# Pinning ScalarE's operand splits behind earlier work in layer 0's attention

## The chip, the cores and the metric

The kernel runs on one core of a Trainium2 chip. The metric is the device time of one execution in microseconds. A core has five engines that run at the same time, each through a stream of instructions of its own, in order: TensorE (PE: matmuls, with its weight loads shown as PEld), VectorE (DVE), ScalarE (ACT), GpSimd (POOL) and SyncE (SP), which here issues nearly all DMA transfers. They wait for one another through semaphores. Matmul results land in PSUM, in banks of 512 float32 values per partition; everything else lives in SBUF.

## The reference

Two post-norm decoder layers on a sequence of 1024 positions and a width of 1024. Layer 0 mixes tokens by differential attention, layer 1 by forgetting attention; a gated MLP with a short convolution follows each. The change touches layer 0's attention alone:

```python
q, k, v = jnp.split(x @ w_qkv, 3, axis=-1)
q = apply_rotary(q.reshape(B, S, H, 2, d), cos, sin, PARTIAL_ROT).transpose(0, 2, 3, 1, 4)
k = apply_rotary(k.reshape(B, S, H, 2, d), cos, sin, PARTIAL_ROT).transpose(0, 2, 3, 1, 4)
v = v.reshape(B, S, H, 2 * d).transpose(0, 2, 1, 3)
...
s = jnp.einsum('bhcqd,bhckd->bhcqk', qb, k) * scale
p = masked_softmax(s, causal_mask(start, Q_BLOCK, S))
a = (p[:, :, 0] - lam * p[:, :, 1]).astype(v.dtype)
o = jnp.einsum('bhqk,bhkd->bqhd', a, v)
o = rms_norm(o, subln_g) * (1.0 - lambda_init)
```

There are 8 heads of two score maps each (`d` = 64).

## The kernel before

**Split operands.** Each product runs as three matmuls in a rounded 32-bit format (`mm3`, L99 to L101). For it every operand is split into a high and a low part: ScalarE copies the source into the rounded type (L88), VectorE subtracts that copy from the source (L90). So each split is one ScalarE and one VectorE instruction, and in the profile all splits share these two lines: `wh` and `wl` are the halves of a weight slab, `q` and `t` those of queries and keys, `pt` those of transposed probabilities, `xh` and `xl` those of activations.

**Slabs.** Layer 0's projection weights come as 24 slabs of 128x1024 (three per head: q, k, v), then 8 slabs of the output weight. `ahead(i)` has SyncE fetch slab i into a staging tile `wst` (L108); `ready(i)` splits it (`cut`). There are two `wst` buffers. The second score map's probabilities of each query tile use the same two.

**The attention loop.** `attention` goes over 8 heads (called pairs, since each has two score maps). While a pair's attention runs, the next pair's projection (`project`) is threaded through it as a generator of 48 steps, each one k tile of a matmul group. It takes q, k and v for the two sequence halves in the order (q,0), (k,0), (q,1), (k,1), (v,0), (v,1). `after(n, fn)` puts a piece of work n steps ahead. The steps that matter here, by the order number n and with i = 3p: fetch slab i+2 at n = 1 and i+3 at n = 4; split i+1 three steps after n = 0 begins, i+2 three steps after n = 2, i+3 three steps after n = 5; fetch i+4 at n = 5.

**Rotary.** Projected q and k are evicted to SBUF by ScalarE (L430). SyncE gathers the rotated rows into a small tile (`gather`, L455 and L457), VectorE turns them (`turn`, L464 to L466), SyncE writes them back (L470). Then `halves` splits q (`split_q`) and k (`split_k`), each half-sequence at a time, and SyncE copies parts of the result to where the score matmuls want them (`move`, L265).

**Attention proper.** For each query tile and map: score matmuls (L507, L508), a masked minimum on VectorE (L510), the exponential on ScalarE (L532), and scaling or combination on VectorE (L537, L542). PE transposes the combined probabilities (L1347) into a PSUM bank (`m`, four buffers), the transposed tile is split (`pt`), and `products` multiplies it with V. `diff_values` normalizes (ScalarE L554 to L559 and L577 to L579, VectorE L560 and L581 to L583, PE L567 and L568). `turn_v` transposes the projected V on PE (L476) into another `m` bank.

**What sets the order.** The source is traced in one order. A scheduler then lays each engine's stream out by a model of when operands will be ready, and may put an instruction ahead of others of the same engine that were traced before it. It also hands out the buffers. On the chip each engine follows the stream it was given.

Of the kernel before, what the change touches and what calls it, by code (L numbers as in the profile page):

```python
# [10 lines left out]
F32R = mybir.dt.float32r  # L11
BF16 = mybir.dt.bfloat16
I32 = mybir.dt.int32
AF = mybir.ActivationFunctionType
# [9 lines left out]
NP = 8  # L24
# [14 lines left out]
W_CUT = 3  # L39
# [16 lines left out]
class Trunk:  # L56
# [25 lines left out]
    def tmp(self, dt=F32, pool=None, tag="t", **k):  # L82
        return (pool or self.tp).tile([P, 1024], dt, tag=tag, name=self.nm(tag), **k)

    def split(self, hi, lo, src, scale=None):

        nc = self.nc
        nc.scalar.activation(hi, src, AF.Copy, scale=1.0 if scale is None else scale)  # L88
        if scale is None:
            nc.vector.tensor_tensor(lo, src, hi.bitcast(F32), op=ALU.subtract)  # L90
        else:
            nc.vector.scalar_tensor_tensor(
                lo, src, scale, hi.bitcast(F32), op0=ALU.mult, op1=ALU.subtract)
# [14 lines left out]
        self.nc.sync.dma_start(st, src)  # L108
        return st

    def cut(self, st, alt=None):
        if alt:
            wh, wl = alt
        else:
            wh = self.wp.tile([P, 1024], F32R, tag="wh", name=self.nm("wh"))
            wl = self.wp.tile([P, 1024], F32R, tag="wl", name=self.nm("wl"))
        self.split(wh, wl, st)
        return wh, wl


# [143 lines left out]
        for dst, src in pairs:  # L264
            self.nc.sync.dma_start(dst.bitcast(F32), src.bitcast(F32))  # L265

    def split_q(self, l, par, src, scale, sl, lo):


        a, b = par[0][:, sl], par[1][:, sl]  # L270
        self.split(a, lo, src, scale)
        hi = slice(0, 64) if l else slice(64, P)
        lo_ = slice(64, P) if l else slice(0, 64)
        self.move((b[hi], a[64:]), (b[lo_], lo[64:]), (a[64:], lo[:64]))

    def split_k(self, l, p, t, src, sl):


        a, b, lo = t[2][:, sl], t[3][:, sl], t[4][:, sl]
        self.split(a, lo, src)  # L280
        self.move((b[64:], a[64:]), (b[:64], a[64:]), (a[64:], a[:64]))
        if l:
            self.move((t[7][:64, sl], lo[64:]))
            if p:
                self.sum_rows(p, t, sl)
# [25 lines left out]
        if i < len(self.slabs):  # L311
            self.stage[i] = self.fetch(self.slabs[i])

    def ready(self, i):
        if i < len(self.slabs):
            self.w[i] = self.cut(self.stage.pop(i))

    def first_loads(self):

# [73 lines left out]
    def project(self, l, p, t):  # L393


        dst, r, i = [None] * 3, {}, 3 * p
        order = ((0, 0), (1, 0), (0, 1), (1, 1), (2, 0), (2, 1)) if l == 0 else \
            [(s, c) for s in range(3) for c in range(2)]
        for n, (s, c) in enumerate(order):
            if l == 0:  # L400
                if n in (1, 4):
                    self.ahead(i + 2 + n // 4)
                elif n in (0, 2, 5):
                    self.after(W_CUT, self.ready, i + (1, 0, 2, 0, 0, 3)[n])
                if n == 5 and p < NP - 1:
                    self.ahead(i + 4)
            else:
                (self.ready if c else self.ahead)(i + s + 1)
            if s == 2 and p == NP - 1:
                self.out_ahead(l, c)  # L410
            ps = self.mbank()
            yield from self.dense_steps(ps, *self.w[i + s], c)
            if c == 0 and (l == 0 or s == 2):
                dst[s] = self.tmp()
            self.after(D_EV, self.result, l, p, s, c, ps, dst[s], t)
            if l == 0 and s == 1:
                self.after(D_EV + 1, self.gather, dst, r, c)
                self.after(D_ROT[c], self.turn, dst, r, c)
                for j in range(2):
                    self.after(D_CUT[c][j], self.halves, dst, t, c, j)  # L420
            if s == 2:
                self.after(D_V[c], self.turn_v, l, c, dst[2], *t[5:7], True)
            if c:
                del self.w[i + s]
# [13 lines left out]
    def halves(self, dst, t, c, j):  # L438

        sl = slice(c * 512, c * 512 + 512)  # L440
        if j == 0:
            self.split_q(0, t[:2], dst[0][:, sl], None, sl, dst[0][:, sl].bitcast(F32R))
        else:
            self.split_k(0, 0, t, dst[1][:, sl], sl)

    def gather(self, dst, r, c):

# [1112 lines left out]
```

## Time and profile before

| what | value |
|---|---|
| median of 3 runs | 2461.72 us (2459.13 to 2468.21) |
| profiled execution, its own time | 2468.86 us |
| its span, first to last instruction | 2467.1 us |
| mean granted TensorE clock | 0.994 |
| layer 0's attention with projections | about the first 500 us |
| ScalarE, VectorE busy over the span | 51%, 78% |

A row of the timeline gives start and duration in us, engine, source line, operation, tiles written and read, shapes and the count of merged instructions. In brackets stands how long the engine was idle before it and what ended that idle time. A row of waits gives the waiter, what it waited for, the total in us, how often, and the longest. A row of windows gives the stretch, its length, the busy time of each engine, the granted clock, the share of the DMA engines and GB/s. Matmuls are pipelined, so that their durations overlap: their rate is read from start to start.

### The profile page before, as it was taken

The numbers are of one execution on the slowest core, as the hardware profiler recorded it, in microseconds if no ns is written. First come the engines' busy times: TensorE is split into PE (matmuls) and PEld (weight loads), VectorE is DVE, ScalarE is ACT, GpSimd is POOL, SyncE is SP. The second block draws the span as 40 slices with busy tenths as digits, with TensorE's granted clock in tenths as the row PEclk, the third lists the DMA queues.
The fourth block names the chain that finished last, engine by engine and source line by source line (L and its number), as shares of the span: only waits on it lengthen the run. The fifth ranks groups of instructions, "written<-read, shape, count | busy, mean of one in ns | idle before, by whom it ended". The sixth has DMA issues, their size and how long they took to land.

```text
span 2467.1 us, 33672 instructions
## 1 busy us (share of the span) xinstructions
PE 2415.5 (98%) x11803; PEld 2016.3 (82%) x11803; DVE 1919.3 (78%) x3763; ACT 1263.7 (51%) x2420; POOL 140.4 (6%) x321
## 2 busy tenths in 40 slices
PE   8999999999999999999999999999999999999998
PEld 6888887788888888888778888888888888888886
DVE  5887777899867667887858777778898667678877
ACT  4565565656544444544535555555465444445444
POOL 2111111001000000000101000000010000000000
PEclk9999999999999999999999999999999999999999
DMA  5232222622322323975232222225223222328751
GB/s 174 72 84 81 73 74 74 196 94 95 103 77 79 99 80 98 341 249 171 88 98 65 65 65 65 65 74 171 78 86 111 77 77 79 101 97 325 257 171 69
DMA packets 116035, 283.41 MB, mean 115 GB/s; under 512 B 18108, under 2 KB 25276, under 8 KB 115864
## 3 DMA queue, kind: packets, MB, share of 16 engines
q1 hardware_dynamic: 115064, 279.34, 35.3%
q8 instruction: 93, 1.52, 0.3%
q0 software_dynamic: 800, 1.90, 0.2%
q14 instruction: 78, 0.64, 0.1%
HBM read 188.44 MB, written 59.18 MB: 100 GB/s over the span
## 4 chain that ended last, share of the span: by engine, by line
PE 75%; DVE 10%; DMA 6%; ACT 4%; SPq 2%; issue 2%; DVEq 0%; POOL 0%; ACTq 0%
PE m L99 18%; PE m L101 18%; PE m L100 18%; PE s L99 3%; PE s L100 3%; PE s L101 3%; PE m L1347 3%; DMA wst<-in_w 3%; PE s L508 2%; PE s L507 2%; DVE s L510 1%; DMA pt<-in_wd 1%; PE m L1373 1%; PE m L1372 1%; ACT wh L88 1%
## 5 line engine op out<-in xcount | busy, mean ns | idle before, releaser
L99 PE MATMUL m<-xh,wh 128*128 128x512 f32 x768 | 320.5, 417 | 10.4 <-ACT xh L88 9.2
L101 PE MATMUL m<-xh,wl 128*128 128x512 f32 x768 | 306.5, 399 | 0.5 <-DVE wl L90 0.5
L100 PE MATMUL m<-xl,wh 128*128 128x512 f32 x768 | 304.0, 396 | 0.0
L99 PE MATMUL m<-xh,wo 128*128 128x512 f32 x656 | 255.6, 390 | 1.1 <-DVE xl L90 0.9
L100 PE MATMUL m<-xl,wo 128*128 128x512 f32 x656 | 255.2, 389 | 0.0
L101 PE MATMUL m<-xh,wo 128*128 128x512 f32 x656 | 255.2, 389 | 0.0
L510 DVE CUSTOM_DVE_ANT_0 s<-s,mask 128x128 f32<-128x128 f32 (+7 forms) x256 | 194.3, 759 | 41.4 <-PE s L508 40.5
L88 ACT ACTIVATE wo<-wg 128x512 fp32r<-128x512 f32 x168 | 106.3, 633 | 223.4 <-PE m L101 215.2
L88 ACT ACTIVATE pt<-m 128x512 fp32r<-128x512 f32 (+1 forms) x240 | 128.7, 554 | 121.7 <-PE m L1347 87.2
L99 PE MATMUL m<-q,wo 128*128 128x512 f32 x472 | 184.0, 390 | 0.0
L100 PE MATMUL m<-q,wo 128*128 128x512 f32 x472 | 183.6, 389 | 0.0
L101 PE MATMUL m<-q,wo 128*128 128x512 f32 x472 | 183.6, 389 | 0.0
L99 PEld LDWEIGHTS m<-xh,wh 128*128 128x128 f32 x768 | 146.5, 191 | 33.8 <-ACT xh L88 9.2
L101 PEld LDWEIGHTS m<-xh,wl 128*128 128x128 f32 x768 | 146.2, 190 | 32.9 <-DVE wl L90 1.6
L90 DVE TENSOR_TENSOR pt<-m,pt 128x512 fp32r<-128x512 f32 (+1 forms) x240 | 148.6, 633 | 21.4 <-ACT pt L88 19.4
L100 PEld LDWEIGHTS m<-xl,wh 128*128 128x128 f32 x768 | 147.1, 192 | 22.2 <-DVE xl L90 0.4
L88 ACT ACTIVATE wo<-t 128x512 fp32r<-128x512 f32 x132 | 82.7, 627 | 140.6 <-PE m L101 133.3
L502 POOL CAST qz<-q 64x128 fp32r<-64x128 f32 x256 | 97.8, 383 | 879.8 <-PE s L508 849.5
L99 PEld LDWEIGHTS m<-xh,wo 128*128 128x128 f32 x656 | 123.1, 188 | 27.6 <-PE m L939 1.4
L90 DVE TENSOR_TENSOR wo<-wg,wo 128x512 fp32r<-128x512 f32 x168 | 115.3, 687 | 38.0 <-ACT wo L88 37.2
L101 PEld LDWEIGHTS m<-xh,wo 128*128 128x128 f32 x656 | 123.1, 188 | 25.8
L100 PEld LDWEIGHTS m<-xl,wo 128*128 128x128 f32 x656 | 123.1, 188 | 25.4
(337 smaller groups left out, 6052.6 us busy)
## 6 DMA issues: line engine op xcount, KB each, us to landing
wst<-in_w SPq DMA_DIRECT2D x46, 512.0 KB
t<-in_wi SPq DMA_DIRECT2D x44, 512.0 KB
ha<-ad SPq DMA_DIRECT2D x88, 256.0 KB
wg<-in_wi SPq DMA_DIRECT2D x42, 512.0 KB
ad<-t SPq DMA_DIRECT2D x42, 512.0 KB
q<-q SPq DMA_DIRECT2D x128, 128.0 KB
pt<-in_wd SPq DMA_DIRECT2D x24, 512.0 KB
hb<-in_wd SPq DMA_DIRECT2D x44, 256.0 KB
```

Of the source, the lines that this page charges most:

```text
L88: nc.scalar.activation(hi, src, AF.Copy, scale=1.0 if scale is None else scale)
L90: nc.vector.tensor_tensor(lo, src, hi.bitcast(F32), op=ALU.subtract)
L99: mm(out, wh, xh, start=start, stop=False)
L100: mm(out, wh, xl, start=False, stop=False)
L101: mm(out, wl, xh, start=False, stop=stop)
L502: nc.gpsimd.tensor_copy(qz[r:r + 64, :], q[r:r + 64, qt * P:qt * P + P])
L507: nc.tensor.matmul(sb[:, ks], q[:, qt * P:qt * P + P], kd[:, ks], start=True, stop=False)
L508: nc.tensor.matmul(sb[:, ks], qz[rows], kl[rows, ks], start=False, stop=True)
L510: nc.vector.tensor_tensor_reduce(sb[:, :ln], sb[:, :ln], self.mask[:, S - ln:], 1.0, BIG, ALU.add, ALU.min, mn)
L1347: nc.tensor.transpose(tb[:, w:w + P], self.pts[q][:, kt * P:kt * P + P], k.ident)
L1372: mm(o, self.v[0][:, vs], h, start=first, stop=False)
L1373: mm(o, self.v[0][:, vs], l, start=False, stop=last)
```

## The change

The helper `split` can now pin its ScalarE instruction: an ordering edge, with no semaphore, to the ScalarE instruction traced just before it. The scheduler can then no longer put it ahead of that one. Pinned are, in layer 0's `project`, the three slab splits of each pair, and the q and k splits of `halves`. The fetch of slab i+4 moves from n = 5 itself to one step after the split of slab i+3 is due. For the last pair, the split of its first output slab (i+3) is traced at n = 5 at once and stays unpinned.

```diff
-    def split(self, hi, lo, src, scale=None):
+    def split(self, hi, lo, src, scale=None, pin=False):
...
-        nc.scalar.activation(hi, src, AF.Copy, scale=1.0 if scale is None else scale)
+        i = nc.scalar.activation(hi, src, AF.Copy, scale=1.0 if scale is None else scale)
+        if pin:
+            self.tc.keep_in_program_order(i)
...
-    def ready(self, i):
+    def ready(self, i, pin=False):
         if i < len(self.slabs):
-            self.w[i] = self.cut(self.stage.pop(i))
+            self.w[i] = self.cut(self.stage.pop(i), pin=pin)
...
             if l == 0:
                 if n in (1, 4):
                     self.ahead(i + 2 + n // 4)
+                elif n == 5 and p == NP - 1:
+                    self.ready(i + 3)
                 elif n in (0, 2, 5):
-                    self.after(W_CUT, self.ready, i + (1, 0, 2, 0, 0, 3)[n])
-                if n == 5 and p < NP - 1:
-                    self.ahead(i + 4)
+                    self.after(W_CUT, self.ready, i + (1, 0, 2, 0, 0, 3)[n], True)
+                    if n == 5:
+                        self.after(W_CUT + 1, self.ahead, i + 4)
...
         if j == 0:
-            self.split_q(0, t[:2], dst[0][:, sl], None, sl, dst[0][:, sl].bitcast(F32R))
+            self.split_q(0, t[:2], dst[0][:, sl], None, sl, dst[0][:, sl].bitcast(F32R), True)
         else:
-            self.split_k(0, 0, t, dst[1][:, sl], sl)
+            self.split_k(0, 0, t, dst[1][:, sl], sl, True)
```

`cut`, `split_q` and `split_k` only pass `pin` on. The edit adds four lines, so that later lines have numbers higher by 2 or 4 (L88 stays, L90 becomes L92, L430 becomes L434, L510 becomes L514).

The scheduler lays the streams out anew. Three places of one pair, the one that starts at about 291 us of the trace before; the others look alike.

First, ScalarE around the normalization and the splits of the first half. `q_623` and `q_625` are the high parts of q and k, `wh_752` (then `wh_751`) is the high part of slab i+3. Before:

```order
L577 ACTIVATE m_690_3397<-m_690_3397,eps_rms_315 128x256
L88 ACTIVATE q_623_3129<-t_676_3337 128x512
L578 ACTIVATE m_690_3397<-m_690_3397 128x256
L579 ACTIVATE sr_719_3530<-m_690_3397 128x256
L88 ACTIVATE q_625_3131<-t_700_3439 128x512
L88 ACTIVATE wh_752_3741<-wst_734_3636 128x1024
L554 COPY of_691_3404<-m_724_3564 128x256
```

Now:

```order
L558 COPY of_691_3404<-m_724_3564 128x256
L536 ACTIVATE p_740_3674,ls_730_3603<-s_728_3596,nm_729_3601 128x896
L562 ACTIVATE m_724_3564<-of_691_3404 128x256
L434 ACTIVATE t_700_3439<-m_720_3540 128x512
L563 CAST sq_733_3616<-m_724_3564 128x256
L88 ACTIVATE q_623_3129<-t_676_3337 128x512
L88 ACTIVATE q_625_3131<-t_700_3439 128x512
L88 ACTIVATE pt_745_3702<-m_741_3676 128x512
L536 ACTIVATE wst_747_3708,ls_738_3669<-s_736_3662,nm_737_3667 128x896
L88 ACTIVATE pt_757_3759<-m_748_3710 128x512
L434 ACTIVATE t_749_3720<-m_735_3638 128x512
L88 ACTIVATE wh_751_3739<-wst_734_3636 128x1024
```

The two splits moved behind the copy, an exponential, an eviction and the cast; the slab's split, which stood just ahead of the copy, now stands eleven rows behind it.

Second, ScalarE around the split of slab i+4 (`wh_785`) and the splits of the second half. Before:

```order
L577 ACTIVATE m_724_3564<-m_724_3564,eps_rms_315 128x256
L88 ACTIVATE wh_785_3871<-wst_750_3721 128x1024
L578 ACTIVATE m_724_3564<-m_724_3564 128x256
L579 ACTIVATE sr_762_3774<-m_724_3564 128x256
L88 ACTIVATE pt_774_3820<-m_761_3770 128x384
L88 ACTIVATE q_623_3129<-t_676_3337 128x512
L532 ACTIVATE wst_776_3826,ls_756_3753<-s_754_3746,nm_755_3751 128x1024
L88 ACTIVATE q_625_3131<-t_700_3439 128x512
```

Now they stand here, eleven rows and more further on, in the start of the next pair:

```order
L88 ACTIVATE pt_790_3882<-m_783_3858 128x512
L563 CAST sq_784_3864<-m_756_3752 128x256
L88 ACTIVATE wh_785_3871<-wst_762_3779 128x1024
L88 ACTIVATE pt_798_3912<-m_793_3890 128x512
L536 ACTIVATE p_800_3919,ls_789_3881<-s_787_3876,nm_788_3879 128x256
L88 ACTIVATE q_623_3129<-t_676_3337 128x512
L536 ACTIVATE wst_807_3958,ls_796_3904<-s_794_3899,nm_795_3902 128x256
```

The slab's split stands between the cast and the next probability split, and q's behind the exponential after that.

Third, VectorE ahead of the low part `pt_774`, whose PSUM bank the V transposes on PE reuse. Before:

```order
L465 TENSOR_TENSOR t_702_3450<-t_702_3450,rope_229 128x256
L464 TENSOR_TENSOR t_702_3450<-t_702_3450,rope_229 128x256
L90 TENSOR_TENSOR pt_758_3761<-m_748_3710,pt_758_3761 128x512
L466 TENSOR_TENSOR t_702_3450<-t_702_3450 128x256
L535 RECIPROCAL rs_775_3823<-ls_744_3701 128x1
L537 TENSOR_SCALAR p_760_3768<-p_760_3768,rs_775_3823 128x1024
L90 TENSOR_TENSOR wl_786_3872<-wst_750_3721,wh_785_3871 128x1024
L510 ISA s_754_3746,nm_755_3751<-s_754_3746,mask_294 128x1024
L510 ISA nm_755_3751 128x1
L90 TENSOR_TENSOR pt_774_3820<-m_761_3770,pt_774_3820 128x384
```

Now:

```order
L92 TENSOR_TENSOR pt_757_3759<-m_748_3710,pt_757_3759 128x512
L469 TENSOR_TENSOR t_702_3450<-t_702_3450,rope_229 128x256
L92 TENSOR_TENSOR wl_752_3740<-wst_734_3636,wh_751_3739 128x1024
L468 TENSOR_TENSOR t_702_3450<-t_702_3450,rope_229 128x256
L539 RECIPROCAL rs_775_3823<-ls_744_3701 128x1
L470 TENSOR_TENSOR t_702_3450<-t_702_3450 128x256
L514 ISA s_753_3744,nm_754_3749<-s_753_3744,mask_294 128x1024
L514 ISA nm_754_3749 128x1
L541 TENSOR_SCALAR p_759_3766<-p_759_3766,rs_775_3823 128x1024
L92 TENSOR_TENSOR pt_774_3820<-m_760_3768,pt_774_3820 128x384
```

The low part of slab i+4 is gone from here, that of slab i+3 has come in, the probability split ahead of the rotary steps has moved up, and the minimum now stands ahead of the scaling.

More of the change, by code (lines that the diff above doesn't have):

```diff
@@ L109, in fetch, with cut @@
         return st
-    def cut(self, st, alt=None):
+    def cut(self, st, alt=None, pin=False):
         if alt:
@@ L116, in cut @@
             wl = self.wp.tile([P, 1024], F32R, tag="wl", name=self.nm("wl"))
-        self.split(wh, wl, st)
+        self.split(wh, wl, st, pin=pin)
         return wh, wl
@@ L265, in move, with split_q @@
             self.nc.sync.dma_start(dst.bitcast(F32), src.bitcast(F32))
-    def split_q(self, l, par, src, scale, sl, lo):
+    def split_q(self, l, par, src, scale, sl, lo, pin=False):
         a, b = par[0][:, sl], par[1][:, sl]
-        self.split(a, lo, src, scale)
+        self.split(a, lo, src, scale, pin)
         hi = slice(0, 64) if l else slice(64, P)
@@ L274, in split_q, with split_k @@
         self.move((b[hi], a[64:]), (b[lo_], lo[64:]), (a[64:], lo[:64]))
-    def split_k(self, l, p, t, src, sl):
+    def split_k(self, l, p, t, src, sl, pin=False):
         a, b, lo = t[2][:, sl], t[3][:, sl], t[4][:, sl]
-        self.split(a, lo, src)
+        self.split(a, lo, src, pin=pin)
         self.move((b[64:], a[64:]), (b[:64], a[64:]), (a[64:], a[:64]))
```

## The prediction

> **What bounds the kernel now.** I read the page's first table first: TensorE (PE) is busy nearly all the time.
>
> ```profile
> PE 2415.5 (98%) x11803; PEld 2016.3 (82%) x11803; DVE 1919.3 (78%) x3763; ACT 1263.7 (51%) x2420; POOL 140.4 (6%) x321
> ```
>
> So a change in ScalarE's order is worth what PE idles or is slowed in layer 0's attention. Next, PE's waits in the first 600 us (total us, times, longest us):
>
> ```profile
> PE m L476 <- DVE pt L90: 15.5, 5, 3.2
> PE m L99 <- ACT xh L88: 9.2, 1, 9.2
> PE m L1347 <- DVE pt L90: 2.3, 4, 0.7
> ```
>
> One wait returns five times: PE is about to transpose the first half of V (L476), and the PSUM bank for it is freed by VectorE's half of a probability split (pt, L90). Then busy time by pair of heads (columns: stretch, length, busy us of PE, PEld, DVE, ACT, POOL, granted clock, DMA):
>
> ```profile
> 113.50:170.10 56.60, 55.60 (x305) 47.22 (x304) 46.16 (x114) 35.77 (x82) 7.99 (x16) 1.00 0.32 89
> 170.10:230.00 59.90, 56.72 (x305) 48.56 (x304) 46.42 (x114) 35.79 (x82) 6.67 (x16) 0.97 0.28 76
> 230.00:291.60 61.60, 57.91 (x306) 49.58 (x305) 46.28 (x115) 35.59 (x82) 7.10 (x16) 0.94 0.26 73
> 291.60:351.10 59.50, 56.32 (x305) 48.35 (x304) 46.30 (x114) 35.81 (x81) 5.99 (x16) 0.97 0.27 76
> 351.10:411.70 60.60, 56.69 (x305) 48.44 (x304) 46.32 (x114) 35.75 (x82) 7.03 (x16) 0.97 0.27 75
> 411.70:474.90 63.20, 58.95 (x306) 50.04 (x305) 50.37 (x122) 39.47 (x90) 5.08 (x16) 0.95 0.52 149
> ```
>
> The first of these pairs runs without the wait and at full clock: 56.60 us. The next four have the same matmuls and take 60.4 on average. After each long wait the clock halves, which two stretches behind the wait of the fourth row, and one around a shorter wait elsewhere, show:
>
> ```profile
> 333.90:337.10 3.20, 3.13 (x10) 2.65 (x11) 3.06 (x9) 1.85 (x4) 0.00 (x0) 0.50 0.36 81
> 88.50:98.50 10.00, 7.63 (x41) 5.95 (x41) 9.48 (x18) 7.17 (x15) 0.74 (x2) 1.00 0.35 97
> ```
>
> At half clock 3.2 us of work cost 1.6 us more. In the second row PE idles 2.4 us, but in pieces, and the clock stays at 1.00.
>
> Now back from the wait, in the pair of 291.6 (timelines of PE, VectorE, ScalarE, SyncE):
>
> ```profile
> 333.97 1.12 PE L476 MATMUL m<-ident,t 128*128 128x128 f32 x4 [3.18 <-DVE pt L90]
> ...
> 328.13 0.49 DVE L466 TENSOR_TENSOR t<-t 128x256 f32<-128x256 f32 x1
> 328.54 0.15 DVE L535 RECIPROCAL rs<-ls 128x1 f32<-128x1 f32 x1
> 328.72 0.75 DVE L537 TENSOR_SCALAR p<-p,rs 128x1024 f32<-128x1024 f32 x1
> 331.08 1.23 DVE L90 TENSOR_TENSOR wl<-wst,wh 128x1024 fp32r<-128x1024 f32 x1 [1.61 <-ACT wh L88]
> 332.22 1.23 DVE L510 CUSTOM_DVE_ANT_0 s<-s,mask 128x1024 f32<-128x1024 f32 x1
> 333.37 0.55 DVE L90 TENSOR_TENSOR pt<-m,pt 128x384 fp32r<-128x384 f32 x1
> ...
> 317.50 1.06 ACT L88 ACTIVATE wh<-wst 128x1024 fp32r<-128x1024 f32 x1 [3.33 <-DMA wst<-in_w]
> ...
> 324.73 0.60 ACT L430 ACTIVATE t<-m 128x512 f32<-128x512 f32 x1
> ...
> 329.99 1.06 ACT L88 ACTIVATE wh<-wst 128x1024 fp32r<-128x1024 f32 x1 [2.03 <-DMA wst<-in_w]
> ...
> 326.11 0.53 SPq L108 DMA_DIRECT2D wst<-in_w  x1
> ```
>
> The slab's DMA is issued at 326.11 and lands at 329.99. Its split stands in ScalarE's stream as if it had landed earlier: ScalarE is blocked 2.03 us, VectorE's half (wl) 1.61 us, and behind wl stand the score minimum (L510) and the pt that PE needs. PE was ready at 333.97 - 3.18 = 330.79. An earlier slab blocks ScalarE 3.33 us in the same pair. Among ScalarE's waits from 113 to 475 us:
>
> ```profile
> ACT wh L88 <- DMA wst<-in_w: 26.5, 10, 4.1
> ```
>
> **The change part by part.** No arithmetic is added or removed; the fetch of slab i+4 is traced four steps later, and its SyncE row still stands directly behind the rotary gathers. What moves is the splits.
>
> *Slabs.* The split that blocked 3.33 us now follows L430 at 324.73, 7 us after its landing at 317.50. The one that blocked 2.03 us moves past the wait, into the next pair, behind the square's cast. That cast, like the next pair's rows here, stands at:
>
> ```profile
> 342.17 0.36 ACT L559 CAST sq<-m 128x256 fp32r<-128x256 f32 x1
> 342.74 0.60 ACT L88 ACTIVATE pt<-m 128x512 fp32r<-128x512 f32 x1 [0.21 <-PE m L1347]
> ...
> 350.33 0.48 PE L99 MATMUL m<-xh,wh 128*128 128x512 f32 x1
> ```
>
> Issued near 326.4 (below) and 3.9 us under way, its slab lands near 330.3, over 8 us ahead of the cast even when the cast comes 3 us earlier. Split by 345, it is first needed by the matmul of 350.33. So both blocks of ScalarE go, at no cost of their own.
>
> *What sets the pt now.* VectorE's row of pt now has this ahead of it: minimum (L510), the pt of the tile before, one rotary multiply, wl, the other multiply, reciprocal, the rotary add, minimum, scaling (L537), pt. The chain starts from
>
> ```profile
> 325.10 1.23 DVE L510 CUSTOM_DVE_ANT_0 s<-s,mask 128x1024 f32<-128x1024 f32 x1
> 326.24 0.14 DVE L510 DVE_READ_ACCUMULATOR2_ANT nm<- 128x1 f32 x1
> 326.24 0.42 DVE L465 TENSOR_TENSOR t<-t,rope 128x256 f32<-128x256 f32 x1
> 327.18 0.42 DVE L464 TENSOR_TENSOR t<-t,rope 128x256 f32<-128x256 f32 x1 [0.52 <-DMA t<-t]
> 327.52 0.68 DVE L90 TENSOR_TENSOR pt<-m,pt 128x512 fp32r<-128x512 f32 x1
> ```
>
> I put its start at 325.3, 0.2 later than before, since the q and k splits of the first half (two on VectorE, 0.68 each) now stand ahead of it, where VectorE waited before. From start to start of the rows above: minimum 1.14, pt 0.61, multiply 0.34, wl 1.14, multiply 0.34, reciprocal 0.18, add 0.41, minimum 1.15, scaling 0.75, pt 0.55: 6.6 us. So pt ends at 331.9, and PE, ready at 330.8, waits **1.1 us instead of 3.18**. The five waits average 15.5 / 5 = 3.1 us, so in four pairs that gains 4 x 2.0 = **8.0 us**. Bounds: no wait at all, 12.4 us; 2.5 us of it left, 2.4 us.
>
> *Clock.* The four pairs' clock shares cost 0.03 x 59.9 + 0.06 x 61.6 + 0.03 x 59.5 + 0.03 x 60.6 = 9.1 us, of which about 1 falls inside the waits. I take **8 us** as gained, since waits of about 1 us left the clock at 1.00 above; the other bound is nothing. [...]
>
> *The last pair* keeps one block, because its first output slab is cut unpinned, as before. Of its long wait and its clock (3.1 us, and 0.05 x 63.2 = 3.2 us) I expect less than half to go, **2.5 us**; bounds 0 and 6.3.
>
> *What the moved work collides with.* In the next pair's start VectorE gets wl (1.23) and later the second half's two splits (0.68 each), ScalarE 1.06 + 2 x 0.63, ahead of two pt splits.
>
> ```profile
> 337.00:350.00 13.00, 13.00 (x86) 11.82 (x85) 10.27 (x33) 8.82 (x23) 1.85 (x6) 1.00 0.30 81
> ```
>
> VectorE is idle 2.7 of these 13 us and takes on 2.6. The pt of 342.74 ends some 1.6 us later, about when PE, whose transposes moved behind six products, wants its bank. I charge 0.3 us for each of five pairs, **1.5 us**; bounds 0 and, if none of the 2.6 is hidden, 13.
>
> *SyncE.* The q and k moves now stand behind ScalarE's later splits and ahead of the last gathers. They issue one after the other, about 0.6 us each:
>
> ```profile
> 318.22 0.39 PE L101 MATMUL m<-xh,wl 128*128 128x512 f32 x1
> ...
> 320.01 0.60 ACT L430 ACTIVATE t<-m 128x512 f32<-128x512 f32 x1
> ...
> 321.51 0.66 SPq L455 DMA_DIRECT2D t<-t  x1
> 322.35 0.50 SPq L265 DMA_DIRECT2D q<-q  x1
> ...
> 324.79 1.22 SPq L457 DMA_DIRECT2D t<-t  x2
> ```
>
> Before, the first gather of the second operand started at 321.51, its data there at 320.6, and ScalarE's block had made that late: PE had it at 318.6. Now this gather starts near 319.4, and twelve issues with their waits end near 326.4, against 326.0. The gather lands near 327.6; the multiply that reads it comes at 328.5. Cost 0; without that cover, one for one.
>
> **Sum.** 8.0 + 8 + 2.5 - 1.5 = 17.0 us. The profiled execution took 2468.86 us (span 2467.1, and 1.8 around it), so its like would take 2451.9. The median of the three runs is 2461.72, 7.1 below it. From there it would be 2444.7. Two of the five half-clock stretches of the profiled run are double ones, by the 0.94 and 0.95 rows; a faster run probably has fewer of them to lose, so I forecast **2446 us**.
>
> **The rivals.**
>
> *The wait survives (30%).* VectorE has 6.6 us of work between a fixed start and PE's need. If the start or a row slips by 1.5 us, the wait is again over 2.5 us and the clock still drops. For it: VectorE is busy 15 of the 20 us ahead of this wait, and the gather's landing has under 1 us of margin. Against: both blocks on ScalarE were the wait's last cause. Gain 5 x 0.7 us: 2458.
>
> ```profile
> 313.90:333.90 20.00, 16.90 (x88) 14.03 (x86) 15.08 (x30) 10.96 (x22) 1.29 (x4) 0.99 0.39 108
> ```
>
> *The clock does not recover (7%).* Waits shorten as forecast, but several short waits for banks still halve the clock: then 8.0 + 1 - 1.5 = 7.5 us is left, 2454. The row 88.50:98.50 speaks against it. [...]
>
> *The wait vanishes (13%).* If VectorE reaches pt by 330.8, the five waits (15.5) and their clock (9.1 + 3.2) go: 27.8 less some 2 of overlap, 2436. For it: the pair at 113.50 already runs so. Against: the 6.6 us have no idle time in them.
>
> *SyncE's queue turns against it (8%).* Place: the last gathers, behind moves that wait for pinned splits and for each other's landings. VectorE is in order, so a gather that is late by x us blocks the minimum and pt behind it. The wait becomes 1.1 - 0.9 + x; from x = 3 us it equals the old one, and at x = 6 (three more waits of a move for another's landing, about 2 us each) it is 6.2 instead of 3.1: 5 x 3.1 = 15 us slower, 2477. Against: the moves before waited only 2.3 us in all here.
>
> ```profile
> SPq L265 <- DMA q<-q: 2.3, 1, 2.3
> ```
>
> That the pins do nothing is excluded by the order.
>
> **How the numbers follow.** Forecast 42%, rivals 30, 7, 13 and 8. The range 2435 to 2461 takes in the vanished wait, the forecast, and the surviving wait; outside lie the slow case and tails. About 0.5% (12.3 us, below 2449.4 or above 2474) is what a measurement here can tell from no change. Faster: the vanished wait (0.13), nine tenths of the forecast (0.38) and a little of the two rivals with a smaller gain (0.05): 0.56. Slower: most of SyncE's rival, 0.07. The rest, 0.37, is the same.
>
> **What will show it.** Right: PE's wait at the V transposes near 1 us, granted clock 1.00 in all these pairs, pairs near 56.6, and no long wait of a slab split for its DMA except in the last pair. Wrong: PE waiting over 2.5 us there, VectorE's rotary multiply waiting for a gather, or a new wait at the probability transposes early in a pair.

## The result and the profile after

The changed kernel takes **2445.47 us** (median of 4 runs, 2442.78 to 2448.64), the kernel before 2462.89 us on the same chip (4 runs, 2459.13 to 2468.21). The ratio is **0.9928, 95% interval 0.9905 to 0.9951**: 17.4 us faster. The forecast was 2446 us. The profiled execution took 2448.64 us, with a span of 2446.8.

TensorE has 9.4 us less to do, by the first table of the page after; it ran the same matmuls in less half-clock time (mean granted clock 0.998, before 0.994):

```profile
PE 2406.1 (98%) x11803; PEld 2007.9 (82%) x11803; DVE 1917.5 (78%) x3763; ACT 1264.2 (52%) x2420; POOL 139.7 (6%) x321
```

Busy time by pair of heads, after, cut at the second V transposes of each pair (columns as in the table of before: stretch, length, busy us of PE, PEld, DVE, ACT, POOL, granted clock, DMA):

```profile
114.18:169.12 54.94, 54.94 (x305) 47.05 (x304) 46.03 (x114) 35.83 (x82) 7.06 (x16) 1.00 0.33 92
169.12:224.08 54.96, 54.96 (x306) 47.04 (x304) 46.13 (x115) 35.86 (x82) 7.05 (x16) 1.00 0.30 82
224.08:279.02 54.94, 54.94 (x305) 47.06 (x304) 46.07 (x114) 35.83 (x82) 7.03 (x16) 1.00 0.30 82
279.02:333.94 54.92, 54.92 (x305) 47.04 (x304) 46.02 (x115) 35.85 (x82) 7.05 (x16) 1.00 0.30 82
333.94:388.91 54.97, 54.97 (x305) 47.06 (x304) 46.06 (x115) 35.84 (x82) 7.06 (x16) 1.00 0.29 82
388.91:449.86 60.95, 58.00 (x307) 49.01 (x306) 51.33 (x120) 38.71 (x86) 6.04 (x17) 0.97 0.45 144
```

In the first five rows length and PE's busy time are equal: PE does not wait at all, and the clock is 1.00. The four pairs that took 59.9, 61.6, 59.5 and 60.6 us take 54.9 to 55.0, and the pair that I had called free of the wait (56.6) also loses 1.7. Of PE's waits between 113 and 475 us only these are left (total us, times, longest us):

```profile
PE m L480 <- DVE pt L92: 2.9, 1, 2.9
PE m L101 <- DVE q L92: 0.6, 1, 0.6
```

The 2.9 us is the last pair's. The blocks of ScalarE on input slabs are gone from its list of waits; for a weight slab it now waits only in the last pair and behind it, for output slabs (6.9 us, against 4.5 before):

```profile
ACT wh L88 <- DMA wst<-in_wo: 6.9, 3, 4.2
```

Where the time went shows best in two stretches: the six pairs, and all behind them. First two rows of before, then two of after, then two of a second profiled execution of the changed kernel (the first experiment of the second group below):

```profile
113.55:474.89 361.34, 342.12 (x1825) 292.17 (x1824) 281.80 (x686) 218.14 (x494) 39.87 (x96) 0.97 0.32 90
474.89:2467.10 1992.21, 1972.35 (x9494) 1641.98 (x9492) 1561.54 (x2887) 984.61 (x1798) 79.39 (x176) 1.00 0.36 118
```

```profile
114.18:449.86 335.68, 332.73 (x1827) 284.26 (x1826) 281.64 (x685) 217.93 (x491) 41.30 (x97) 0.99 0.33 95
449.86:2446.80 1996.94, 1973.27 (x9492) 1641.39 (x9490) 1561.36 (x2889) 985.62 (x1801) 80.08 (x175) 1.00 0.36 119
```

```profile
113.51:447.59 334.08, 331.20 (x1828) 283.04 (x1826) 281.47 (x685) 218.33 (x491) 42.30 (x97) 1.00 0.33 95
447.59:2440.00 1992.41, 1972.84 (x9492) 1641.53 (x9490) 1561.63 (x2889) 985.54 (x1801) 80.09 (x175) 1.00 0.36 119
```

The six pairs go from 361.34 to 335.68 us, **25.7 us**; of that, PE's idle time (length less busy) falls from 19.2 to 2.9 us, 16.3, and the other 9.4 is the clock. The first profile after then lost 4.7 us behind the pairs, which the second did not: that is a difference between executions, not the change. How 25.7 us in two profiles and 17.4 us in the medians go together is taken up below.

The chain that PE used to wait for, in the pair that the prediction followed (timelines of VectorE and PE after):

```profile
311.03 1.23 DVE L514 CUSTOM_DVE_ANT_0 s<-s,mask 128x1024 f32<-128x1024 f32 x1
...
312.18 0.69 DVE L92 TENSOR_TENSOR pt<-m,pt 128x512 fp32r<-128x512 f32 x1
312.78 0.41 DVE L469 TENSOR_TENSOR t<-t,rope 128x256 f32<-128x256 f32 x1
313.75 1.23 DVE L92 TENSOR_TENSOR wl<-wst,wh 128x1024 fp32r<-128x1024 f32 x1 [0.55 <-ACT wh L88]
314.89 0.42 DVE L468 TENSOR_TENSOR t<-t,rope 128x256 f32<-128x256 f32 x1
...
317.49 0.55 DVE L92 TENSOR_TENSOR pt<-m,pt 128x384 fp32r<-128x384 f32 x1
...
318.10 0.66 PE L480 MATMUL m<-ident,t 128*128 128x128 f32 x4
```

pt ends at 318.04 and PE transposes at 318.10 without a wait. The chain takes 7.0 us from the minimum at 311.03, and it starts 7.07 us ahead of PE.

### The profile page after: what moved, and what is told of

The parts are those of the page before. It is cut to its first block, busy times and chain, and to the rows that moved or that the text cites. A ratio compares the mean times of both kernels' runs of the same rounds, so it can differ in the third digit from the quotient of the medians.

```text
span 2446.8 us, 33670 instructions
## 1 busy us (share of the span) xinstructions
PE 2406.1 (98%) x11803; PEld 2007.9 (82%) x11803; DVE 1917.5 (78%) x3763; ACT 1264.2 (52%) x2420; POOL 139.7 (6%) x321
## 4 chain that ended last, share of the span: by engine, by line
PE 81%; DVE 8%; DMA 6%; ACT 3%; issue 1%; SPq 1%; DVEq 0%; POOL 0%; ACTq 0%; POOLq 0%
PE m L101 20%; PE m L103 20%; PE m L102 20%; PE m L1351 3%; PE s L101 3%; PE s L102 3%; PE s L103 3%; PE s L512 3%; PE s L511 2%; PE m L1377 1%; PE m L1376 1%; DMA pt<-in_wd 1%; DVE wo L92 1%; DMA wb<-in_wd 1%; DMA t<-od 1%
## 5 line engine op out<-in xcount | busy, mean ns | idle before, releaser
L514 DVE CUSTOM_DVE_ANT_0 s<-s,mask 128x128 f32<-128x128 f32 (+7 forms) x256 | 194.3, 759 | 39.0 <-PE s L512 37.6
L88 ACT ACTIVATE wo<-wg 128x512 fp32r<-128x512 f32 x168 | 106.4, 633 | 226.2 <-PE m L103 216.4
L88 ACT ACTIVATE pt<-m 128x512 fp32r<-128x512 f32 (+1 forms) x240 | 128.5, 553 | 131.1 <-PE m L1351 96.8
L92 DVE TENSOR_TENSOR pt<-m,pt 128x512 fp32r<-128x512 f32 (+1 forms) x240 | 148.4, 632 | 20.1 <-ACT pt L88 17.6
L88 ACT ACTIVATE wo<-t 128x512 fp32r<-128x512 f32 x132 | 82.8, 627 | 140.6 <-PE m L103 133.2
L92 DVE TENSOR_TENSOR wo<-wg,wo 128x512 fp32r<-128x512 f32 x168 | 115.2, 687 | 39.8 <-ACT wo L88 38.9
```

Of the source, the lines that this page charges most:

```text
L88: i = nc.scalar.activation(hi, src, AF.Copy, scale=1.0 if scale is None else scale)
L514: nc.vector.tensor_tensor_reduce(sb[:, :ln], sb[:, :ln], self.mask[:, S - ln:], 1.0, BIG, ALU.add, ALU.min, mn)
```

## The experiments

For the first four kernels, theory A is that the splits that block ScalarE on a slab that has not landed carry the gain, and theory B that the query and key splits, or what stands in VectorE's chain, carry it. The later kernels have theories of their own, which stand with each. No kernel here leaves out any of the computation; one repeats a subtraction. Each group shares its runs of the kernel before: median 2463.39 us for the first four kernels (14 runs), 2458.99 for the next four (9 runs), 2458.84 for the last four (19 runs). "Faster by" is that median less the kernel's. The ratio is not the quotient of the two medians: by it the first kernel gains 5.9 us instead of 8.0, and the others differ by at most 1.6 us. "Six pairs" is the length of the stretch above in the kernel's own profile, between the same marks.

| kernel | median us | ratio to before (95%) | faster by | six pairs |
|---|---|---|---|---|
| slab pins alone | 2455.35 | 0.9976 (0.9963–0.9989) | 8.0 | 348.6 |
| q and k pins alone | 2454.14 | 0.9960 (0.9945–0.9975) | 9.3 | 345.2 |
| slab i+4's pin alone | 2448.40 | 0.9937 (0.9923–0.9952) | 15.0 | 341.8 |
| slab i+3's pin alone | 2457.41 | 0.9973 (0.9961–0.9985) | 6.0 | 349.3 |
| the change again | 2441.48 | 0.9933 (0.9920–0.9945) | 17.5 | 334.1 |
| the change, last pair pinned too | 2438.43 | 0.9920 (0.9907–0.9932) | 20.6 | 332.6 |
| the change less slab i+3's pin | 2448.66 | 0.9963 (0.9950–0.9976) | 10.3 | 341.6 |
| the change, VectorE's subtraction three times | 2448.03 | 0.9956 (0.9943–0.9970) | 11.0 | 339.8 |
| the fetch moved, no pin | 2462.11 | 1.0015 (1.0004–1.0026) | -3.3 | 354.5 |
| the change, q and k pins in the first half | 2445.95 | 0.9954 (0.9939–0.9968) | 12.9 | 338.1 |
| the change, q and k pins in the second half | 2453.32 | 0.9979 (0.9969–0.9989) | 5.5 | 346.6 |
| the change, slab splits a step earlier | 2444.52 | 0.9948 (0.9933–0.9963) | 14.3 | 338.1 |

**Slab pins alone.** The change without the pins on queries and keys:

```diff
-            self.split_q(0, t[:2], dst[0][:, sl], None, sl, dst[0][:, sl].bitcast(F32R), True)
+            self.split_q(0, t[:2], dst[0][:, sl], None, sl, dst[0][:, sl].bitcast(F32R))
-            self.split_k(0, 0, t, dst[1][:, sl], sl, True)
+            self.split_k(0, 0, t, dst[1][:, sl], sl)
```

> The slab splits of the change stay pinned, the q and k splits are free again and go back ahead of the normalization; the moved fetch and the last pair stay as in the change. Theory A (the two slab splits that block ScalarE carry the gain): 14 to 18 us faster than before, the wait at the V transposes under 1 us in the four middle pairs, granted clock 1.00 there. Theory B (VectorE's load ahead of the wait carries it, so the q and k splits must leave that stretch too): the second half's q and k splits stand right behind the wait and the first half's back in idle time, so the gain is under 8 us and a wait over 1.5 us is left.

8.0 us faster by the medians and 5.9 by the ratio, about half of what A needs and near B. The slab blocks are gone, and yet PE waits 1.8 to 2.1 us in five of the six pairs, 0.6 in the first. PE's waits of this kernel in the first 600 us, then VectorE's and PE's timeline in the pair that was followed:

```profile
PE m L480 <- DVE pt L92: 10.4, 6, 2.1
```

```profile
317.57 1.23 DVE L514 CUSTOM_DVE_ANT_0 s<-s,mask 128x1024 f32<-128x1024 f32 x1 [0.26 <-PE s L512]
...
319.99 0.43 DVE L469 TENSOR_TENSOR t<-t,rope 128x256 f32<-128x256 f32 x1 [1.13 <-issue]
321.12 0.43 DVE L468 TENSOR_TENSOR t<-t,rope 128x256 f32<-128x256 f32 x1 [0.70 <-DMA t<-t]
321.46 0.68 DVE L92 TENSOR_TENSOR pt<-m,pt 128x512 fp32r<-128x512 f32 x1
...
326.25 0.55 PE L480 MATMUL m<-ident,t 128*128 128x128 f32 x3 [1.94 <-DVE pt L92]
```

The two rotary multiplies (L469, L468) stand ahead of the 512-wide pt here, and VectorE idles 1.83 us ahead of them: 0.70 us for a gather's data, 1.13 for nothing that the profile shows. In the change that pt stands first and fills this time. The minimum starts 6.7 us ahead of PE's readiness, about as in the change, but the chain takes 8.6 us instead of 7.0. That is a new wait in place of the old one, and A alone does not explain the gain.

**Query and key pins alone.** The kernel before with the last two lines of the change, and nothing else:

```diff
-            self.split_q(0, t[:2], dst[0][:, sl], None, sl, dst[0][:, sl].bitcast(F32R))
+            self.split_q(0, t[:2], dst[0][:, sl], None, sl, dst[0][:, sl].bitcast(F32R), True)
-            self.split_k(0, 0, t, dst[1][:, sl], sl)
+            self.split_k(0, 0, t, dst[1][:, sl], sl, True)
```

> Only the q and k splits are pinned; slabs, fetch and last pair are as before. Theory A: both blocks of ScalarE stay, so the long wait stays at 3 us or more in each pair with its half clock: within 6 us of before, rather slower, since the first half's q and k splits now fill time in which VectorE waited. Theory B: at least 8 us faster.

9.3 us faster: A as stated falls here, and B's 8 us is met. Nine of the ten blocks are still there (first row: ScalarE's waits from 113 to 475 us; then timelines), but the scheduler, which plans around pins, has put the blocked split of slab i+4 behind sr, and PE's transposes now wait, in the four middle pairs, for a bank that sr frees:

```profile
ACT wh L88 <- DMA wst<-in_w: 23.7, 9, 3.4
```

```profile
323.68 1.06 ACT L88 ACTIVATE wh<-wst 128x1024 fp32r<-128x1024 f32 x1 [1.66 <-DMA wst<-in_w]
...
324.07 0.41 DVE L584 SCALAR_TENSOR_TENSOR sr<-m,sr 128x256 f32<-128x256 f32 x1
324.77 1.23 DVE L92 TENSOR_TENSOR wl<-wst,wh 128x1024 fp32r<-128x1024 f32 x1 [0.29 <-ACT wh L88]
...
324.54 0.55 PE L478 MATMUL m<-ident,t 128*128 128x128 f32 x3 [1.14 <-DVE sr L584]
```

PE's waits at the V transposes fall from 15.5 to 9.3 us in all, 3.6 of it still for pt. So here a block costs less, since what frees PE's bank stands ahead of it.

**One slab split at a time.** No query or key pin, and only the split of slab i+4 (traced at n = 0 of the next pair) or of slab i+3 pinned (the second kernel has `n == 5` in the line below):

```diff
-                    self.after(W_CUT, self.ready, i + (1, 0, 2, 0, 0, 3)[n], True)
+                    self.after(W_CUT, self.ready, i + (1, 0, 2, 0, 0, 3)[n], n == 0)
```

> Of all splits only that of slab i+4 is pinned, so the block of 2.0 us is gone and the block of 3.3 us stays. Theory A with the last cause alone: VectorE's chain loses 1.6 us of waiting and 1.2 us of wl ahead of the pt, 2.8 of the 3.2 us of wait, the clock stays full: 14 to 18 us faster. If the earlier block sets the start of the chain as well, 1 to 2 us of wait remain: 10 to 14 us faster, clock 1.00. Theory B: under 5 us.

> Of all splits only that of slab i+3 is pinned, so the block of 3.3 us is gone and that of 2.0 us, last ahead of the wait, stays. Theory A with the last cause alone: wait near 3 us, half clock as before, within 4 us of before. If the earlier block delays the gathers and through SyncE the fetch of the next slab, that slab lands 1 to 2 us earlier and the wait falls to 1 to 2 us with full clock: 8 to 14 us faster. Theory B: within 4 us.

15.0 and 6.0 us faster. The first meets A's 14 us; the second lies between A (within 4 us of before) and the 8 to 14 us of an earlier landing. PE's waits in the first 600 us, of the first and of the second:

```profile
PE m L480 <- DVE sr L586: 4.0, 5, 1.1
PE m L480 <- DVE pt L92: 2.8, 1, 2.8
```

```profile
PE m L480 <- DVE pt L92: 12.3, 6, 2.8
```

The split of slab i+4 is the one whose block the prediction saw as the last cause of the wait, and its pin alone removes most of it: no middle wait is over 1.13 us, and the granted clock of the whole span is 0.999, against 0.998 in the first profile after, which has one half-clock stretch in the six pairs. With i+3's pin alone the waits stay between 1.4 and 2.8 us. 15.0 + 6.0 is more than the 17.4 of the whole, and slab pins together gave 8.0: the parts do not add. Each kernel's streams differ around the pins, as the scheduler orders the neighbours anew; which of these differences makes up the sum was not taken apart.

**The change again, and the last pair pinned too.** In the second kernel the split of the last pair's first output slab is pinned, and traced three steps later, like the others:

```diff
-                elif n == 5 and p == NP - 1:
-                    self.ready(i + 3)
...
-                    if n == 5:
+                    if n == 5 and p < NP - 1:
```

> The changed kernel once more, as the yardstick of the three variants beside it: 2445.5 measured before, so 2443 to 2448 here, with PE's wait at the first V transposes gone in the four middle pairs and 2.9 us in the last.

> The change, and the first output slab's split in the last pair pinned as well (no unpinned split is left). Theory A (the wait is made by the blocked split, in the last pair as in the others): the last pair's wait of 2.9 us shrinks below 1.5 us and its half-clock stretch of 3.4 us (1.7 us of work lost) goes with it, so 2 to 4 us faster than the change. Theory B (the last pair's wait comes from its additional output slabs, which load ScalarE and VectorE more, 39.5 and 50.4 us against 35.8 and 46.3): the wait stays over 2 us, within 1.5 us of the change.

2441.48 us (2441.05 to 2444.48) and **2438.43 us** (2438.23 to 2439.93), five runs each on one chip: the ranges do not touch, and the second is 3.0 us faster, as A said. It beats both kernels. On this chip the kernel before takes some 4 us less as well, so the miss of the 2443 to 2448 expected for the change is the chip's; the ratio is the old one. In the last pair's trace PE's wait of 2.6 to 2.9 us is gone; its six pairs are

```profile
111.82:444.37 332.55, 331.31 (x1829) 283.40 (x1828) 281.57 (x686) 219.54 (x493) 42.82 (x97) 1.00 0.33 97
```

with 1.2 us of idle PE in all.

**The change without slab i+3's pin.**

```diff
-                    self.after(W_CUT, self.ready, i + (1, 0, 2, 0, 0, 3)[n], True)
+                    self.after(W_CUT, self.ready, i + (1, 0, 2, 0, 0, 3)[n], n != 5)
```

> The change without the pin on the split of slab i+3, which goes back to where VectorE had idle time, so VectorE's subtraction of 1.14 us is no longer in the chain ahead of pt. Theory A (the wait is what VectorE's chain ends later than PE arrives, and never below zero): the chain is already early enough, so shortening it gives nothing in the middle pairs: within 2 us of the change, as long as ScalarE's block on that slab (3 us) does not come back ahead of the q and k splits. Theory B (that split's block costs by itself, as in the kernel before): 4 us or more slower than the change.

7.2 us slower than the change: B of this run. VectorE's subtraction has left the chain, and the chain is late all the same. ScalarE, VectorE and PE in the pair that was followed:

```profile
305.50 1.06 ACT L88 ACTIVATE wh<-wst 128x1024 fp32r<-128x1024 f32 x1 [3.11 <-DMA wst<-in_w]
...
314.52 1.22 DVE L514 CUSTOM_DVE_ANT_0 s<-s,mask 128x1024 f32<-128x1024 f32 x1
...
320.80 0.66 PE L480 MATMUL m<-ident,t 128*128 128x128 f32 x4 [1.27 <-DVE pt L92]
```

PE was ready at 320.80 - 1.27 = 319.53, and the minimum that opens the chain started only 5.0 us ahead of it, against 7.07 in the change. ScalarE's exponential behind the block (306.72) starts 12.8 us ahead of PE's readiness, and the same one in the change (303.21) 14.9. So a block of 3.1 us nine microseconds earlier moves the *start* of the chain by 2 us. The run with slab i+4's pin alone, in which slab i+3's split blocks 2.64 us, lies between: its minimum starts 6.0 us ahead.

**VectorE's subtraction for slab i+3 three times.** The same result, written three times:

```diff
-            nc.vector.tensor_tensor(lo, src, hi.bitcast(F32), op=ALU.subtract)
+            for _ in range(max(1, pin)):
+                nc.vector.tensor_tensor(lo, src, hi.bitcast(F32), op=ALU.subtract)
...
-                    self.after(W_CUT, self.ready, i + (1, 0, 2, 0, 0, 3)[n], True)
+                    self.after(W_CUT, self.ready, i + (1, 0, 2, 0, 0, 3)[n], 3 if n == 5 else True)
```

> The change, with VectorE's subtraction for slab i+3 done three times (same result): two more of 1.14 us stand ahead of pt, and the reciprocal and scaling (0.93 us) go behind it, so pt comes 1.35 us later in the four middle pairs, at an unchanged PE. Theory A (pt ended 0.06 us before PE came, so there is no slack): four waits of about 1.3 us, 5 us slower than the change, clock still 1.00 behind them. Theory B (VectorE has slack that the trace does not show): under 2 us slower, no wait over 0.5 us. Theory C (the wait also halves the clock): 10 us or more slower.

6.5 us slower than the change, near the 5 us of A, with pairs of 55.8 to 56.3 us instead of 54.95. But the time is not lost where A put it. The scheduler moved PE's V transposes seven products later, where they wait for nothing, and the loss appears behind them, at the probability transposes (PE's waits from 113 to 455 us):

```profile
PE m L1352 <- DVE p L547: 2.7, 5, 0.5
PE m L481 <- DVE pt L93: 2.0, 1, 2.0
PE m L1352 <- DVE pt L93: 0.7, 4, 0.2
```

These waits make 3.4 of the 5.5 us by which the first five pairs are longer than those of the change beside it. VectorE is busy about 2.0 us more in a pair (48.1 against 46.05), and the pair is 1.1 us longer: about half of the added work is hidden, so that neither A's "no slack" nor B holds as stated. Some 1.9 us of the loss in the profile lies ahead of the six pairs, at a wait of 2.5 us at 96 us.

**The fetch moved, no pin.**

```diff
-                    self.after(W_CUT, self.ready, i + (1, 0, 2, 0, 0, 3)[n], True)
+                    self.after(W_CUT, self.ready, i + (1, 0, 2, 0, 0, 3)[n])
```

and the query and key pins off as in the first experiment. The last pair's first output slab stays traced early, as in the change.

> The kernel before with the fetch of slab i+4 moved as in the change, and no pin at all. Theory A (the pins carry the gain, the fetch merely goes with them): within 4 us of the kernel before, its blocks of ScalarE and the waits of about 3 us still there. Theory B (the later fetch alone unblocks ScalarE, since the scheduler then puts the split later too): 8 us or more faster than before.

3.3 us slower than before: A. Waits of PE from 100 to 460 us, and blocks of ScalarE from 110 to 460 us, are the old ones:

```profile
PE m L480 <- DVE pt L92: 14.2, 5, 3.1
```

```profile
ACT wh L88 <- DMA wst<-in_w: 24.7, 9, 3.3
```

The later fetch alone gains nothing; the pins are needed. The slab pins without the later fetch were not tried.

**Query and key pins in one half of the rows.** `True` becomes `c == 0` in the first kernel and `c == 1` in the second, here and in the line of split_q:

```diff
-            self.split_k(0, 0, t, dst[1][:, sl], sl, True)
+            self.split_k(0, 0, t, dst[1][:, sl], sl, c == 0)
```

> The change with the query and key splits pinned in the first half of the rows only (the second half's four splits unpinned). Theory A (the first half's pins matter, since they set what stands ahead of pt in VectorE's stream): within 3 us of the change, 14 to 19 us faster than before, and no wait over 1 us at the V transposes. Theory B (the second half's pins matter, since they take the 2.6 us block of ScalarE on a rotary gather out of the way): 6 to 11 us faster than before, like the change without any of these pins (8.0).

> The change with the query and key splits pinned in the second half of the rows only. Theory A (the first half's pins matter): 6 to 11 us faster than before, with a wait of 1 to 2 us at the V transposes in the middle pairs. Theory B (the second half's matter): within 3 us of the change, 14 to 19 us faster than before.

12.9 and 5.5 us faster than before. PE's waits of the first, from 113 to 475 us, and of the second in the first 600 us:

```profile
PE m L480 <- DVE pt L92: 2.3, 1, 2.3
PE m L101 <- DVE acc L824: 2.0, 2, 1.1
```

```profile
PE m L480 <- DVE pt L92: 10.3, 6, 2.9
```

With the first half's pins the middle waits are gone (the 2.3 is the last pair's); with the second half's alone all of them stay (1.3 to 2.0 us in the four middle pairs), and the gain, just under A's 6 us, is no larger than with none of these pins. So it is the first half's pins that matter for the wait. They stand ahead of the chain. The first kernel still misses the 14 us that A wanted, and is 4.5 us slower than the change: the last pair takes 62.1 us instead of 59.4, with time at half clock (a granted clock of 0.97 from 394 to 460 us) and new waits on acc, and the other pairs 0.1 to 0.5 us more each.

**Slab splits a step earlier.**

```diff
-W_CUT = 3
+W_CUT = 2
```

> The change with every pinned slab split (and the fetch) one step earlier, so that the split of slab i+4 stands directly behind the second V eviction, near its landing, and blocks ScalarE there for up to 2 us; the query and key pins stay. Theory A (a block costs only where the pt that PE waits for stands behind it; here it stands behind the V transposes' pt): within 3 us of the change. Theory B (any block of ScalarE of that size costs PE time): 5 us or more slower than the change.

3.0 us slower than the change, at the edge of what A allowed, but this run tells nothing about A or B: the fetch moves with the split, the slab had landed, and no block arose (from 113 to 475 us the only slabs that ScalarE waits for are output slabs, 6.2 us).

## Why the prediction was right, and where it was not

**What bounds the kernel: right.** The long wait at the V transposes for pt, behind a split that waits for its slab, was the loss. With the blocks gone, the wait and the half clock behind it went, and the moved fetch alone does not bring that about.

**"PE waits 1.1 us instead of 3.18", 8.0 us for four pairs: undersized.** The wait is zero in all four, 12.4 us, which was my upper bound. The step that failed is the chain's start, which I held at 325.3, 5.5 us ahead of PE's readiness, "0.2 later than before". It now stands 7.07 us ahead. The block of 3.33 us on slab i+3 had delayed this start too, and the run that puts that block back moves it to 5.0. The length was nearly right (6.6 forecast, 7.0 found): 1.1 - 1.6 + 0.4 is just below zero. The same error stands in the SyncE part, where I let the product at 318.22 end the bank that L430 evicts. By the numbers of the tiles that product writes the next slab's bank, and in the trace it signals nothing; the product at 316.18, which does, had filled the evicted one by 316.6. So ScalarE's block had held up the eviction, and all behind it, by some 2 us more than I allowed.

**"Pairs near 56.6": wrong floor.** The pair that I took as undisturbed had 1.0 us of idle PE in it, most of it in waits of 0.2 to 0.4 us, and the pairs of the change take 54.95. The other 0.65 us is time in which the profile has PE busy (55.60 against 54.95); its cause stays open. The four pairs gained 21.8 us, not the 14.8 that 8.0, 8 and four fifths of the collisions' 1.5 make.

**The clock, 8 us: right.** In the four pairs the half-clock stretches of before are

```profile
214.20:217.61 3.41, 3.41 (x13) 3.02 (x12) 3.33 (x9) 1.42 (x4) 0.29 (x1) 0.50 0.63 143
272.23:279.05 6.82, 5.88 (x20) 5.20 (x21) 5.41 (x15) 3.27 (x7) 0.29 (x1) 0.50 0.42 96
333.67:337.08 3.41, 3.11 (x10) 2.63 (x11) 3.27 (x9) 2.08 (x4) 0.00 (x0) 0.50 0.36 81
395.11:398.52 3.41, 3.41 (x12) 2.75 (x11) 2.53 (x8) 1.59 (x5) 0.09 (x1) 0.50 0.42 96
```

and the change has none there: its four rows have 1.00. PE is busy in 15.8 of these 17.1 us, and half of that, 7.9 us, is my estimate of what they cost at 0.50. Over the six pairs the clock gave 9.4 us by the rows above, against the 8 forecast for the four pairs and a part of the last pair's 2.5. The other bound that I gave, nothing, no run shows: in each of the four pairs of before the long wait is followed by a row at 0.50.

**The last pair, 2.5 us: right** (63.15 to 60.95, 2.2 us; 59.39 in the second profile, 3.8), and its reason is borne out: pinning the one split that was left, and tracing it later, is worth 3.0 us more.

**Collisions, 1.5 us: not there.** PE has no wait early in a pair. PE's transposes and VectorE's pt both moved, and the pairs run without any idle time.

**SyncE, cost 0: right for the change.** The multiply at 314.89 follows its predecessor without a wait. The mechanism of that rival shows in part all the same: without the query and key pins VectorE waits 0.70 us for a gather in the same place, of 1.83 us idle, and half the gain is lost.

**The rivals.** In mechanism it was the third, the wait vanishes, which I gave 13%; its price of 25.8 us meets the 25.7 of the six pairs. Its time of 2436 did not come, because I took those 25.8 us off the median, and the profiled execution of before had more to lose than the median run: it lies 6 to 7 us above the medians. The kernel with only the fetch moved, whose waits are those of before, spent 354.5 us in the six pairs of its profile, not 361.3, with three half-clock stretches of 3.41 us there instead of three single and two double ones. The runs fit this: of the 28 runs of the kernel before that stand beside the last eight kernels, the six with a mean granted clock of 0.995 average 2460.6 us and the five with 0.998 2455.3, and the profiled execution of before had 0.994. From 354.5 to the 334.1 and 335.7 of the change is 19 to 20 us, near the measured 17.4; the last 2 us are not settled. So 2446 against 2445.5 is in part two errors that cancel: a wait term too small by 4.4 us, with nothing for the small waits and 1.5 for collisions that did not come, and a base from which I took the profile's clock losses nearly whole. That the two numbers agree to half a microsecond is luck.

## What to carry to other kernels

When a block of an in-order engine is removed, move the whole chain with it, its start too: here a wait of 3.1 us for a transfer, nine microseconds ahead of the start of the chain, had set when the chain began (5.0 us ahead of PE's readiness with it, 7.07 without). Take a pair as the floor only if the bottleneck engine is busy for its whole length (here PE was busy in 55.60 of the 56.60 us, and pairs of 54.95 came). Where a scheduler plans around pins, the parts of such a change do not add, so each combination has to be timed, and so has the step that the change leaves out (here the last pair's pin).

## What the runs showed of the clock that was not expected

The half-clock stretches in the rows above last 3.41 us, and the two double ones of the profile before, at 272.23 and 456.55 us, 6.82. In the 3.41 us ahead of each stretch of that profile (starts at 214.20, 272.23, 333.67, 395.11 and 456.55 us) PE idled 2.00, 2.25, 2.87, 2.79 and 2.39 us; ahead of the one in the first profile after, at 434.07, 1.99. The double stretches had 0.94 and 0.53 us of idle time in their first 3.41 us, the single ones of the two profiles 0.00, 0.30, 0.00 and 0.00. Two cases that lie close together stand in the profile of the slab pins alone (two pairs of successive windows; length less PE's busy time is the idle time, and the granted clock the third number from the end):

```profile
323.50:326.91 3.41, 1.47 (x9) 0.99 (x8) 3.38 (x9) 0.85 (x2) 0.00 (x0) 1.00 0.15 39
326.92:330.33 3.41, 3.41 (x9) 2.64 (x9) 2.35 (x6) 1.87 (x4) 0.00 (x0) 0.50 0.46 103
381.53:384.94 3.41, 1.58 (x9) 0.97 (x8) 3.38 (x7) 1.62 (x3) 0.00 (x0) 1.00 0.17 48
384.95:388.36 3.41, 3.41 (x21) 3.02 (x22) 3.39 (x11) 2.45 (x6) 0.29 (x1) 1.00 0.45 103
```

The window behind 1.94 us of idle time ran at 0.50, the one behind 1.83 at 1.00. The length of a wait alone did not decide: this wait of 1.94 us was followed by 0.50, the longer one of 2.6 us in the last pair of the second profile of the change left the granted clock of the six pairs at 1.00. In the first profile the same wait took 2.9 us, 1.99 of it in the 3.41 us ahead of the stretch, and 0.50 followed. In the stretch from 434.07 products of 512 columns start 0.42 us apart (434.88 and 435.30 us), and the same two kinds, behind it, 0.23 (444.91 and 445.14). So I estimate the cost of a stretch of 3.41 us that PE fills at half of it, 1.7 us. What else decides where the clock falls to 0.50, these rows do not show.
